# Fourteen Strassen blocks in place of eight plain ones in the first group of the second MLP

## Chip, cores and metric

The kernel runs on one core of a Trainium2 chip. The metric is the device time of one execution in microseconds; its median over three runs is shown, and one execution was profiled.

## The reference

A trunk of two layers works on 256 tokens of 2048 channels in float32. Layer 0 mixes by causal pooling, layer 1 by stick-breaking attention over shared keys and values; each ends in the same kind of MLP, with 8192 hidden channels, and the change concerns the MLP of layer 1.

```python
def rms_norm(x, g):
    xf = x.astype(jnp.float32)
    y = xf * lax.rsqrt(jnp.mean(xf * xf, axis=-1, keepdims=True) + EPS)
    return (y * g.astype(jnp.float32)).astype(x.dtype)

def squared_relu_mlp(x, w_up, w_down):
    h = jax.nn.relu(jnp.einsum('bsd,df->bsf', x, w_up))
    return jnp.einsum('bsf,fd->bsd', h * h, w_down)

def reference(...):
    for layer in range(DEPTH):
        if layer < N_A:
            x = x + multiscale_pool_mixer(rms_norm(x, pool_norm[layer]), pool_w[layer],
                                          pool_scale[layer])
        else:
            ...
            x = x + jnp.einsum('bsd,de->bse', o, w_o[j])
        x = x + squared_relu_mlp(rms_norm(x, mlp_norm[layer]), w_up[layer], w_down[layer])
    return rms_norm(x, final_norm)
```

## The kernel before

**Blocks and splits.** All weights pass through the core once, in blocks of 128 partitions x 4 x 512 (1 MB), listed in `order` beforehand. A product in float32 is made of three matmuls of a reduced type: activations and weights are each split into a high part and the rest (high x high, rest x high, high x rest). A block is therefore loaded (`load`), then split (`split`): ScalarE casts it into a tile `hi` (L194), VectorE subtracts that from the block into `lo` (L195). There are three buffers each for `hi` and `lo`, so a split may start when the block three places ahead of it has been multiplied. `next_block` keeps three blocks split and up to six loaded. Plain loads are issued by SyncE (L176) into three buffers `raw` or into one of four tiles `c0`, `c1`, `d0`, `d1`.

**Groups and Strassen's products.** The hidden channels of an MLP are worked in eight groups (`NG`) of 1024. Up-projections of groups 1 to 7 are made by seven products in Strassen's form (Winograd's variant): the 256 tokens and the group's two sets of 512 columns are halved, as are the 2048 input channels, and seven products on sums of quarters take the place of eight. Each product has two parts (input chunks 0 and 1, chunks 2 and 3), each with a block of its own: `P40` is product 4, part 0, and has 12 matmuls. The sums of weights are made while loading: product 4 loads a quarter into `c`; product 5 adds another quarter to it in the memory by an accumulating load, which POOL issues (L182), after product 4's block has been split; product 6 adds `d` to `c` on VectorE (L180); product 3 adds a third quarter by an accumulating load. Product 1 loads into `d`, and product 7 adds to that by an accumulating load. `c0` and `d0` serve part 0, `c1` and `d1` part 1. Product 2 loads a quarter of its own into `raw`. The table says so:

```python
CHAIN = {4: ("c", (1, 1)), 5: ("c", (1, 0)), 6: ("c", None), 3: ("c", (0, 1)),
         1: ("d", (0, 0)), 7: ("d", (1, 0)), 2: (None, (0, 1))}
```

**Group 0** of each MLP is made plainly (`whole`): eight blocks `U`, each with 24 matmuls (12 for each half of the tokens), into banks `x`, `y`, `z`, `turn`. It begins while the norm of input chunk 3 is still being made.

**A group's order** is written out in `stage_plan`. `T` are transposes of the activated hidden channels (four each, from tiles `c11` to `c22` into `ht0`, `ht1`), `D` are blocks of the down-projection of the group before (24 matmuls each). The first six groups of products begin as follows:

```python
        order = ("T0 T1 P40 T2 T3 P41" if g == 1 else "T2 P40 T3 P41 T0") + " P10 "
        order += ("" if g == 1 else "T1 ") + ("P11 D00 D01 P50 P51 D10 P60 P61 D11 D20 P70 P71 D21 "
                                              "P30 P31 D30 P20 P21 D31")
```

A planner places the instructions on each engine's queue at build time: by this order, but letting work that it takes to be ready go ahead of work that it takes to be waiting. On the chip every queue runs in the order so made.

**The norm.** Before the second MLP stands the output projection (16 blocks, `product_a`, L270 to L273). After each of its four chunks the norm's share of this chunk is made (`norm1.take`): squares (L316), transposes (L333), a scaling into a tile `f` (L414), casts and rests of quarters (L419, L420), sums of quarters (L425 to L431). The tiles `f` lie in `c0`, `c1`, `d0`, `c0`; a quarter that only the plain group 0 needs lies in `d1` (`other`). Chunk 3 is taken after the first block of group 0. The relu in the hidden channels scales by the token's factor (L492, L532).

Of the kernel before, what the change touches and what calls it, by code (L numbers as in the profile page):

```python
# [9 lines left out]
F32 = mybir.dt.float32  # L10
# [7 lines left out]
P = 128  # L18
# [3 lines left out]
NB = 512  # L22
NCH = D // NB
# [30 lines left out]
         1: ("d", (0, 0)), 7: ("d", (1, 0)), 2: (None, (0, 1))}  # L54


def stage_plan(g):


    if g == 0:  # L60
        order = "U000 U010 U001 U011 U100 U101 U110 U111"
    elif g < NG:
        order = ("T0 T1 P40 T2 T3 P41" if g == 1 else "T2 P40 T3 P41 T0") + " P10 "
        order += ("" if g == 1 else "T1 ") + ("P11 D00 D01 P50 P51 D10 P60 P61 D11 D20 P70 P71 D21 "
                                              "P30 P31 D30 P20 P21 D31")
        if g == NG - 1:
            order = order.replace("D11 D20 P70 P71 D21 P30 P31 D30 P20 P21 D31",
                                  "D11 P70 P71 D20 P30 P31 D21 P20 P21 D30")
    else:
        order = "T0 T1 E31 T2 T3 D00 D01 D10 D11 D20 D21 D30 D31"  # L70
    return [(s[0], *map(int, s[1:])) for s in order.split()]
# [3 lines left out]
def trunk_kernel(ctx: ExitStack, tc: tile.TileContext, xt_in, band, cols, pool_w, up_w, down_w,  # L75
# [60 lines left out]
    def mlp_blocks(layer):  # L136
        for g in range(NG + 1):
            last = {}
            for what, a, *b in stage_plan(g):
                if what in "DE":  # L140
                    block(down_w[layer, g - 1 - (what == "E"), a, b[0]])
                elif what == "U":
                    block(up_w[layer, g, a, b[0], b[1]])
                elif what == "P":
                    tag, at = CHAIN[a]
                    src = f"d{b[0]}" if at is None else up_w[layer, g, *at, b[0]]
                    last[a, b[0]] = block(src, tag=tag and f"{tag}{b[0]}", add=a in (5, 6, 3, 7),
                                          after=last[6, b[0]] if a == 7 else None)
# [58 lines left out]
    def next_block():  # L207
        while state["split"] < min(state["used"] + SPLITS, len(order)):
            split()
        while state["loaded"] < min(state["used"] + LOADS, len(order)):  # L210
            load()
        state["used"] += 1
        return ready.pop(0)
# [165 lines left out]
    class Fast(Norm):  # L379

        def __init__(self, gain, new_bank, homes):
            super().__init__()
            self.gain, self.new_bank, self.pools = gain, new_bank, []
            self.f, self.homes = [None] * NCH, homes

        def release(self):
            while self.pools:
# [5 lines left out]

        def quarters(self, n, src=None):

            if n == 0:
                self.other = wide("d1", F32R).rearrange("p n (l k s) -> p n l k s", l=2, k=2)
            pool = tc.alloc_tile_pool(name=f"fast{n}", bufs=1, side="right", reuse_waits="tile")  # L400
            self.pools.append(pool)
            hi = pool.tile([P, PARTS, 2, P], F32R, name="fh")
            lo = pool.tile([P, PARTS, 2, P], F32R, name="fl")
            self.parts[n] = (hi, lo)

            f = self.f[n] = wide(self.homes[n]).rearrange("p a (b k s) -> p (a b) k s", b=2, k=2)
            for half in range(2):
                if src is None:
                    bank = self.turned(n, half, (0, 1))
                for k in range(2):  # L410
                    c = 2 * half + k
                    x = bank[:, :, k, :] if src is None else src[:, c, :].rearrange(
                        "p (t s) -> p t s", t=NT)
                    nc.scalar.activation(out=f[:, 2 * half:2 * half + 2, k, :], in_=x, func=AF.Copy,  # L414
                                         scale=gt[:, self.gain, n * KT + c:n * KT + c + 1])
            for h, l, x in ((hi[:, 0], lo[:, 0], f[:, 0]),
                            (self.other[:, n, 0], self.other[:, n, 1], f[:, 1]),
                            (hi[:, 1:3], lo[:, 1:3], f[:, 2:4])):
                nc.scalar.copy(out=h, in_=x)  # L419
                nc.vector.tensor_tensor(out=l, in0=x, in1=h.bitcast(F32), op=ALU.subtract)  # L420

# [27 lines left out]
    def mlp(layer, norm, following, ps_s):  # L449

        with ExitStack() as later_pools:
# [8 lines left out]
            bank, u, h = {}, {}, {}  # L460
            r = None

            def product(i, part):

                name = {1: "x", 6: "x", 7: "x", 5: "y", 3: "y", 2: "z", 4: "z"}[i]
                begins = part == 0 and i in (1, 5, 2, 4)
                if begins:
                    bank[name] = ps_s.tile([P, NB], F32, name=name)
# [2 lines left out]
                for kg in range(2):  # L471
                    fh, fl = norm.parts[2 * part + kg]
                    for k in range(2):
                        ah, al = fh[:, SLOT[i], k, :], fl[:, SLOT[i], k, :]
                        wh, wl = hi[:, 2 * kg + k, :], lo[:, 2 * kg + k, :]
                        ends = part == 1 and kg == 1 and k == 1
                        nc.tensor.matmul(b, lhsT=ah, rhs=wh, start=begins and kg == 0 and k == 0,  # L477
                                         stop=False, skip_group_check=True)
                        nc.tensor.matmul(b, lhsT=al, rhs=wh, start=False, stop=False,  # L479
                                         skip_group_check=True)  # L480
                        nc.tensor.matmul(b, lhsT=ah, rhs=wl, start=False, stop=ends,  # L481
                                         skip_group_check=True)
                if part == 0:
                    return

# [80 lines left out]
            for g in range(NG + 1):  # L566
                follow = None
                if g == NG:
                    norm.release()
                    follow = following(new_bank)  # L570
                for what, *at in stage_plan(g):
                    if what == "P":
                        product(*at)
                    elif what == "T":
                        turn(*at, g == NG)
                    elif what == "U":
                        whole(*at)
                    elif what == "E":
                        down(*at)
                    else:  # L580
                        down(*at, follow)
# [3 lines left out]

    ps_s = four_banks(0)
    new_bank = bank_of(ps_s, ("z", "turn"))
    norm = Fast(G["mlp0"], new_bank, ("d0", "c0", "d0", "c1"))
    pools = [tc.alloc_tile_pool(name="xs23", bufs=1, reuse_waits="tile")]
    xs = [pools[0].tile([P, KT, S], F32, name=f"xs{n}") for n in range(2, NCH)]  # L590
    pp = tc.alloc_tile_pool(name="poolmix", bufs=2, reuse_waits="tile")
# [182 lines left out]
    for hg in range(NHG):  # L774
# [86 lines left out]
        product_w(kvq.parts, to_heads(qT, "q"))  # L861
        side.extend([[logs(0)], [logs(1)], [weights(0)], [weights(1)], [mix(0)], [mix(1)]])
        product_a(kvq.parts, to_values)
    norm1 = Fast(G["mlp1"], None, ("c0", "c1", "d0", "c0"))
    last_banks = []

    def end_of_attention():
        attention.close()
        ps_m[0].release()
        last_banks.append(four_banks(1))  # L870
        norm1.new_bank = bank_of(last_banks[0], ("z", "turn"))

    side.append([end_of_attention])
    for n in range(NCH):
# [4 lines left out]
        product_a(oT, added)  # L879
        if n < NCH - 1:  # L880
            norm1.take(n)
    op.release()
    side.append([lambda: norm1.take(NCH - 1)])


    class Last(Norm):
# [127 lines left out]
```

## Time and profile before

| what | us |
|---|---|
| median of three runs (1811.88 to 1813.05) | 1813.01 |
| the profiled execution | 1811.7 |
| its span, first to last instruction | 1810.0 |
| TensorE (PE) busy | 1797.5 |
| VectorE (DVE) busy | 1292.4 |
| ScalarE (ACT) busy | 1069.6 |
| GpSimd (POOL) busy | 92.5 |

Time lies mostly in the matmuls; a stage is read by cutting windows out of the span. The output projection ends at 1118.0 us of the span, group 0 of the second MLP runs to 1162.4, and each later group takes about 84 us.

### The profile page before, as it was taken

To read this page: it belongs to the slowest core of one execution; us is meant where nothing else is said; L and a number is where in the kernel's file an instruction comes from. 1 tells how busy PE (TensorE), PEld (TensorE's weight loads), DVE (VectorE), ACT (ScalarE), POOL (GpSimd) and SP (SyncE) were. 2 spreads that over 40 slices of the span, in tenths; PEclk is the share of its full clock that TensorE was granted. 3 is DMA by queue.
4 is the path that set the end of the run, shared out by engine and by line. 5 is a ranking of instruction groups with operands and counts; after the bars stand their busy time and mean duration, and the time that the engine had idled before them with its cause. 6 is when DMAs were issued, how large, how long until landed. Compare 5 with 4: busy or idle time off the path is not lost.

```text
span 1810.0 us, 20830 instructions
## 1 busy us (share of the span) xinstructions
PE 1797.5 (99%) x8348; PEld 1480.6 (82%) x8348; DVE 1292.4 (71%) x1098; ACT 1069.6 (59%) x1089; POOL 92.5 (5%) x125
## 2 busy tenths in 40 slices
PE   9999999999999999999999999999999999999998
PEld 4888888888888888888888888888888888888886
DVE  6577877877786876676766666577787868787863
ACT  5665665756565665565665555556565656566553
POOL 0000000000000100000000100000000101000000
PEclk9999999999999999999999999999999999999999
DMA  7678888897979874555445456797979798888851
GB/s 274 234 184 299 207 285 242 252 264 221 279 212 308 198 232 164 186 170 179 163 165 184 163 175 239 212 258 232 278 210 300 198 299 202 296 208 285 209 210 70
DMA packets 57553, 404.85 MB, mean 224 GB/s; under 512 B 6512, under 2 KB 6512, under 8 KB 9328
## 3 DMA queue, kind: packets, MB, share of 16 engines
q1 hardware_dynamic: 44784, 314.39, 47.7%
q0 software_dynamic: 12096, 88.09, 25.5%
q8 instruction: 65, 1.06, 0.2%
q10 hardware_dynamic: 576, 1.05, 0.2%
q14 instruction: 32, 0.26, 0.0%
HBM read 401.40 MB, written 2.10 MB: 223 GB/s over the span
## 4 chain that ended last, share of the span: by engine, by line
PE 98%; issue 1%; ACT 0%; DMA 0%; DVE 0%; SPq 0%; POOL 0%; ACTq 0%; POOLq 0%
PE bank L272 16%; PE bank L273 16%; PE bank L270 16%; PE bank L236 7%; PE x L477 4%; PE x L479 4%; PE x L481 4%; PE bank L241 3%; PE z L481 3%; PE z L477 3%; PE z L479 3%; PE y L481 3%; PE y L479 3%; PE y L477 3%; PE bank L683 2%; PE turn L545 1%
## 5 line engine op out<-in xcount | busy, mean ns | idle before, releaser
L195 DVE TENSOR_TENSOR lo<-raw,hi 128x2048 fp32r<-128x2048 f32 x188 | 430.6, 2290 | 247.4 <-ACT hi L194 246.9
L194 ACT CAST hi<-raw 128x2048 fp32r<-128x2048 f32 x188 | 359.6, 1913 | 305.8 <-PE bank L272 224.3
L272 PE MATMUL bank<-hi,ht 128*128 128x512 f32 x1024 | 399.9, 391 | 0.0
L273 PE MATMUL bank<-lo,ht 128*128 128x512 f32 x1024 | 399.3, 390 | 0.0
L270 PE MATMUL bank<-hi,ht 128*128 128x512 f32 x1024 | 399.3, 390 | 0.0
L195 DVE TENSOR_TENSOR lo<-c,hi 128x2048 fp32r<-128x2048 f32 x112 | 256.4, 2289 | 53.0 <-ACT hi L194 53.0
L194 ACT CAST hi<-c 128x2048 fp32r<-128x2048 f32 x112 | 214.6, 1916 | 126.4 <-PE bank L272 43.9
L272 PEld LDWEIGHTS bank<-hi,ht 128*128 128x128 f32 x1024 | 192.3, 188 | 44.0 <-DVE ht L550 4.6
L270 PEld LDWEIGHTS bank<-hi,ht 128*128 128x128 f32 x1024 | 192.3, 188 | 39.6
L273 PEld LDWEIGHTS bank<-lo,ht 128*128 128x128 f32 x1024 | 192.2, 188 | 39.4
L201 DVE SCALAR_TENSOR_TENSOR lo<-raw,gt,hi 128x512 fp32r<-128x512 f32 x192 | 135.4, 752 | 79.4 <-ACT hi L200 78.9
L200 ACT ACTIVATE hi<-raw,gt 128x512 fp32r<-128x512 f32 x192 | 126.0, 714 | 95.6 <-PE bank L236 48.5
L194 ACT CAST hi<-d 128x2048 fp32r<-128x2048 f32 x56 | 107.2, 1914 | 87.9 <-PE bank L272 67.2
L195 DVE TENSOR_TENSOR lo<-d,hi 128x2048 fp32r<-128x2048 f32 x56 | 128.3, 2292 | 42.7 <-ACT hi L194 42.7
L477 PE MATMUL x<-hi,fh 128*128 128x512 f32 x336 | 132.0, 393 | 0.0
L479 PE MATMUL x<-hi,fl 128*128 128x512 f32 x336 | 131.9, 393 | 0.0
L481 PE MATMUL x<-lo,fh 128*128 128x512 f32 x336 | 131.2, 390 | 0.0
L559 DVE TENSOR_TENSOR xr<-bank,xr 128x512 f32<-128x512 f32 x128 | 87.8, 686 | 39.8 <-PE bank L273 39.2
L182 POOL DMA_DIRECT2D c<-in_up_w x56 | 48.5, 866 | 875.8 <-DVE lo L195 829.8
L236 PE MATMUL bank<-d,hi 128*128 128x512 f32 x256 | 90.6, 398 | 0.0
L477 PE MATMUL z<-hi,fh 128*128 128x512 f32 x224 | 89.5, 400 | 0.0
L236 PE MATMUL bank<-c,hi 128*128 128x512 f32 x256 | 88.9, 395 | 0.0
(282 smaller groups left out, 2794.9 us busy)
## 6 DMA issues: line engine op xcount, KB each, us to landing
raw<-in_down_w SPq DMA_DIRECT2D x128, 1024.0 KB, 4.9
c<-in_up_w POOLq DMA_DIRECT2D x56, 1024.0 KB, 10.7
raw<-in_up_w SPq DMA_DIRECT2D x44, 1024.0 KB, 5.3
c<-in_up_w SPq DMA_DIRECT2D x28, 1024.0 KB, 5.1
d<-in_up_w SPq DMA_DIRECT2D x28, 1024.0 KB, 8.2
d<-in_up_w POOLq DMA_DIRECT2D x28, 1024.0 KB, 8.8
raw<-in_k_w SPq DMA_DIRECT2D x16, 1024.0 KB, 4.8
raw<-in_q_w SPq DMA_DIRECT2D x16, 1024.0 KB, 4.9
```

The source lines that it names most:

```text
L194: nc.scalar.copy(out=hi, in_=raw)
L195: nc.vector.tensor_tensor(out=lo, in0=raw, in1=hi.bitcast(F32), op=ALU.subtract)
L200: nc.scalar.activation(out=hi[:, k, :], in_=raw[:, k, :], func=AF.Copy, scale=gs)
L201: nc.vector.scalar_tensor_tensor(out=lo[:, k, :], in0=raw[:, k, :], scalar=gs, in1=hi[:, k, :].bitcast(F32), op0=ALU.mult, op1=ALU.subtract)
L236: nc.tensor.matmul(banks[j], lhsT=hi[:, k, cols], rhs=a, start=first, stop=last)
L270: nc.tensor.matmul(banks[t], lhsT=a_hi, rhs=hi[:, k, :], start=first and k == 0, stop=False)
L272: nc.tensor.matmul(banks[t], lhsT=a_lo, rhs=hi[:, k, :], start=False, stop=False)
L273: nc.tensor.matmul(banks[t], lhsT=a_hi, rhs=lo[:, k, :], start=False, stop=last and k == KT - 1)
L477: nc.tensor.matmul(b, lhsT=ah, rhs=wh, start=begins and kg == 0 and k == 0, stop=False, skip_group_check=True)
L479: nc.tensor.matmul(b, lhsT=al, rhs=wh, start=False, stop=False, skip_group_check=True)
L481: nc.tensor.matmul(b, lhsT=ah, rhs=wl, start=False, stop=ends, skip_group_check=True)
L559: nc.vector.tensor_tensor(out=chunk(t, n), in0=bank["d"][t], in1=chunk(t, n), op=ALU.add)
```

## The change

`stage_plan` gets the layer, and group 0 of the second MLP becomes fourteen Strassen blocks, part 0 of products 4, 1, 2 and 5 first. Product 2 takes bank `turn` in group 0, since `z` is still in use by product 4. `product` pops a side task behind each block, as `whole` does, so chunk 3's norm is taken behind `P40`. `next_block` stops loading where an accumulating load would have to wait for a split that isn't listed yet. The norm of the second MLP gets tiles of its own for `f` (`home`, in memory that attention has left, and `home1`, in memory of the attention's output), and doesn't make `other`; chunk 3's transposes go to banks of `ps_w`. The first MLP is as before.

```diff
-def stage_plan(g):
-    if g == 0:
+def stage_plan(layer, g):
+    if g == 0 and layer == 0:
         order = "U000 U010 U001 U011 U100 U101 U110 U111"
+    elif g == 0:
+        order = "P40 P10 P20 P50 P11 P41 P21 P51 P60 P61 P70 P71 P30 P31"
     elif g < NG:
...
         while state["loaded"] < min(state["used"] + LOADS, len(order)):
+            after = order[state["loaded"]][-1]
+            if after is not None and after >= state["split"]:
+                break
             load()
...
-        def __init__(self, gain, new_bank, homes):
+        def __init__(self, gain, new_bank, new_home, whole):
...
-            if n == 0:
+            if n == 0 and self.whole:
                 self.other = wide("d1", F32R).rearrange("p n (l k s) -> p n l k s", l=2, k=2)
...
-            f = self.f[n] = wide(self.homes[n]).rearrange("p a (b k s) -> p (a b) k s", b=2, k=2)
+            f = self.f[n] = self.new_home(n).rearrange("p a (b k s) -> p (a b) k s", b=2, k=2)
...
-            for h, l, x in ((hi[:, 0], lo[:, 0], f[:, 0]),
-                            (self.other[:, n, 0], self.other[:, n, 1], f[:, 1]),
-                            (hi[:, 1:3], lo[:, 1:3], f[:, 2:4])):
+            pieces = [(hi[:, 0], lo[:, 0], f[:, 0]), (hi[:, 1:3], lo[:, 1:3], f[:, 2:4])]
+            if self.whole:
+                pieces.insert(1, (self.other[:, n, 0], self.other[:, n, 1], f[:, 1]))
+            for h, l, x in pieces:
...
-            def product(i, part):
-                name = {1: "x", 6: "x", 7: "x", 5: "y", 3: "y", 2: "z", 4: "z"}[i]
+            def product(i, part, g):
+                name = {1: "x", 6: "x", 7: "x", 5: "y", 3: "y", 2: "z" if g else "turn", 4: "z"}[i]
...
+                after_block()
                 if part == 0:
                     return
...
-    norm1 = Fast(G["mlp1"], None, ("c0", "c1", "d0", "c0"))
-    last_banks = []
+    homes, last_banks = [], []
+    norm1 = Fast(G["mlp1"], None, lambda n: homes[-1].tile([P, KT, NB], F32, name="home"), False)
     def end_of_attention():
...
+        homes.append(tc.alloc_tile_pool(name="home", bufs=1, reuse_waits="tile"))
...
+    homes.pop().release()
     op.release()
-    side.append([lambda: norm1.take(NCH - 1)])
+    def last_taken():
+        later = tc.alloc_tile_pool(name="beside", bufs=1, reuse_waits="tile")
+        later.tile([P, KT, NB], F32, name="beside")
+        homes.append(tc.alloc_tile_pool(name="home1", bufs=1, reuse_waits="tile"))
+        norm1.new_bank = lambda: ps_w.tile([P, NB], F32, name="bank")
+        norm1.take(NCH - 1)
+        homes.pop().release()
+        later.release()
+    side.append([last_taken])
```

## Rows read from the trace of the kernel before

**Rows 1.** The page: busy time of each engine, share of the span, instructions.

```profile
PE 1797.5 (99%) x8348; PEld 1480.6 (82%) x8348; DVE 1292.4 (71%) x1098; ACT 1069.6 (59%) x1089; POOL 92.5 (5%) x125
```

**Rows 2.** Windows: stretch, length, busy us (instructions) by engine, clock, DMA share, GB/s.

```profile
1074.00:1118.00 44.00, 44.00 (x200) 36.22 (x199) 27.90 (x27) 23.19 (x32) 0.00 (x0) 1.00 0.64 230
...
1118.00:1162.40 44.40, 44.40 (x201) 36.87 (x200) 23.59 (x22) 21.92 (x25) 1.75 (x2) 1.00 0.70 231
```

**Rows 3.** Timeline of PE: start, us, engine, line, operation, out<-in, count.

```profile
1118.00 0.39 PE L525 MATMUL x<-hi,fh 128*128 128x512 f32 x1
...
1120.72 0.39 PE L525 MATMUL y<-hi,d 128*128 128x512 f32 x1
...
1123.44 0.60 PE L333 MATMUL z<-ident,xr 128*128 128x128 f32 x4
...
1162.44 0.39 PE L477 MATMUL z<-hi,fh 128*128 128x512 f32 x1
...
1164.96 0.66 PE L545 MATMUL turn<-ident,c 128*128 128x128 f32 x4
...
1168.58 0.48 PE L481 MATMUL z<-lo,fh 128*128 128x512 f32 x1
```

**Rows 4.** Groups of instructions by line and form, whole span.

```profile
L195 DVE TENSOR_TENSOR lo<-c,hi 128x2048 fp32r<-128x2048 f32 x112 | 256.4, 2289 | 53.0 <-ACT hi L194 53.0
...
L194 ACT CAST hi<-c 128x2048 fp32r<-128x2048 f32 x112 | 214.6, 1916 | 126.4 <-PE bank L272 43.9 <-PE x L479 26.3 <-PE y L479 22.3
...
L180 DVE TENSOR_TENSOR c<-c,d 128x2048 f32<-128x2048 f32 x28 | 64.0, 2286 | 0.4
...
L498 DVE TENSOR_TENSOR c<-y,c 128x512 f32<-128x512 f32 x14 | 9.6, 683 | 0.0
```

**Rows 5.** Timelines of DVE and POOL where group 1 begins.

```profile
1153.48 2.29 DVE L195 TENSOR_TENSOR lo<-c,hi 128x2048 fp32r<-128x2048 f32 x1 [3.15 <-ACT hi L194]
...
1156.07 0.89 POOL L182 DMA_DIRECT2D c<-in_up_w  x1 [126.34 <-DVE lo L195]
```

**Rows 6.** The page's loads: issuing queue, count, KB each, median us to landing.

```profile
c<-in_up_w POOLq DMA_DIRECT2D x56, 1024.0 KB, 10.7
...
c<-in_up_w SPq DMA_DIRECT2D x28, 1024.0 KB, 5.1
```

**Rows 7.** Landing of L182's loads: all, then those issued at 1156.07, 1245.27, 1196.23.

```profile
DMA to landing us min/median/max: 7.9/9.8/18.7
...
DMA to landing us min/median/max: 8.2/8.2/8.2
...
DMA to landing us min/median/max: 10.3/10.3/10.3
...
DMA to landing us min/median/max: 15.0/15.0/15.0
```

**Rows 8.** Timelines of ACT and DVE around the start of group 0.

```profile
1107.09 1.91 ACT L194 CAST hi<-raw 128x2048 fp32r<-128x2048 f32 x1 [2.58 <-PE bank L272]
...
1122.35 0.30 ACT L289 ACTIVATE rows<-total,eps 128x2 f32<-128x2 f32 x1 [1.81 <-DVE total L339]
...
1123.41 1.90 ACT L194 CAST hi<-raw 128x2048 fp32r<-128x2048 f32 x1 [0.52 <-PE y L527]
...
1109.03 2.29 DVE L195 TENSOR_TENSOR lo<-raw,hi 128x2048 fp32r<-128x2048 f32 x1 [2.01 <-ACT hi L194]
...
1119.95 2.29 DVE L195 TENSOR_TENSOR lo<-raw,hi 128x2048 fp32r<-128x2048 f32 x1 [1.07 <-ACT hi L194]
...
1127.89 0.42 DVE L420 TENSOR_TENSOR d<-c,d 128x256 fp32r<-128x256 f32 x1
```

**Rows 9.** Window of chunk 3's norm, VectorE alone: length, busy us (instructions), clock, DMA.

```profile
1122.20:1135.20 13.00, 9.19 (x16) 1.00 0.51 166
```

**Rows 10.** Windows at the end of the span, columns as in rows 2.

```profile
1797.00:1799.50 2.50, 0.00 (x0) 0.00 (x0) 1.12 (x7) 1.22 (x4) 0.00 (x0) 1.00 0.00 0
1799.50:1803.00 3.50, 3.14 (x15) 3.17 (x16) 1.91 (x5) 0.57 (x2) 0.00 (x0) 0.53 0.00 0
```

More of the change, by code (lines that the diff above doesn't have):

```diff
@@ L138, in mlp_blocks @@
             last = {}
-            for what, a, *b in stage_plan(g):
+            for what, a, *b in stage_plan(layer, g):
                 if what in "DE":
@@ L379, in trunk_kernel @@
     class Fast(Norm):
-        def __init__(self, gain, new_bank, homes):
+        def __init__(self, gain, new_bank, new_home, whole):
             super().__init__()
-            self.gain, self.new_bank, self.pools = gain, new_bank, []
-            self.f, self.homes = [None] * NCH, homes
+            self.gain, self.new_bank, self.pools, self.whole = gain, new_bank, [], whole
+            self.f, self.new_home = [None] * NCH, new_home
         def release(self):
@@ L570, in mlp @@
                     follow = following(new_bank)
-                for what, *at in stage_plan(g):
+                for what, *at in stage_plan(layer, g):
                     if what == "P":
-                        product(*at)
+                        product(*at, g)
                     elif what == "T":
@@ L587, in trunk_kernel @@
     new_bank = bank_of(ps_s, ("z", "turn"))
-    norm = Fast(G["mlp0"], new_bank, ("d0", "c0", "d0", "c1"))
+    norm = Fast(G["mlp0"], new_bank, lambda n: wide(("d0", "c0", "d0", "c1")[n]), True)
     pools = [tc.alloc_tile_pool(name="xs23", bufs=1, reuse_waits="tile")]
```

## The prediction

> **What bounds the kernel now.** I read the page first. TensorE is busy for 1797.5 of the 1810.0 us [rows 1], so on the whole only fewer matmuls, or a new wait of TensorE, can move the time. This busy share is a mean, though, and the change touches one stage: group 0 of the second MLP. So I cut the windows there next [rows 2]: TensorE has no gap, VectorE works 23.59 of 44.40 us, ScalarE 21.92. The timeline of TensorE then gives the scale [rows 3]. I call 1118.00 t = 0, the first matmul of the group. The twelve matmuls of one token half take 2.72 us (1118.00 to 1120.72), or 0.227 us each. The eight transposes of chunk 3's norm take 0.8 us. Group 1's first product begins at t = 44.4 (1162.44), and its second ends, four transposes of T0 and of T1 included, at about t = 50.9 (just behind 1168.58). The reader should see that one Strassen block (12 matmuls) occupies TensorE for 2.72 us and one plain block (24) for 5.44.
>
> **The gain.** Eight plain blocks are 192 matmuls, fourteen Strassen blocks 168. The 24 that go are worth 24 x 0.227 = 5.4 us. TensorE alone would end the group at 168 x 0.227 + 0.8 = t = 38.9.
>
> **What is added to the other engines.** Six more blocks have to be split: a cast of 1.92 us on ScalarE, then a subtraction of 2.29 on VectorE [rows 4]. P60 and P61 each add d to c on VectorE, 2.29 us each. Evacuations of the products add four VectorE operations of 0.68, and the dropped quarter saves 0.4. VectorE's work in the stage becomes 23.6 + 6 x 2.29 + 2 x 2.29 + 2.7 - 0.4 = 44.2 us, against 38.9 of TensorE. So VectorE by itself takes back the gain, unless work slides past the group's end. ScalarE comes to 21.9 + 6 x 1.92 = 33.4 us and a few copies, and bounds nothing.
>
> **The waits, which decide.** Six of the new loads are not plain: P50, P51, P70, P71, P30 and P31 add to a tile that an earlier block has just been split from. They can start only when that split has read the tile, and their own split only when they have landed. In group 1 this looks as follows [rows 5]: the subtraction of P40 starts at 1153.48 and ends at 1155.77, and POOL issues the accumulating load of P50 at 1156.07, 0.30 later. Its median time to landing is 10.7 us, while a plain load into c takes 5.1 [rows 6]. Alone it took 8.2, second of a close pair 10.3, third in a row with others beside it 15.0 [rows 7]. From the start of a cast to the end of its subtraction are 4.2 us (1107.09 to 1111.32) [rows 8]. Group 1 and the later groups put some 19 us of other blocks (two products, two down blocks, another product) between P41 and P51. The new list puts P21 alone between them, 2.72 us.
>
> So I follow tile c1 through the group: P41, P51, P61, P31, and then P41 of group 1. A block's third matmul needs the subtraction; ten matmuls, 2.27 us, follow it.
> - P41's split needs the buffers that P20 leaves: t = 3 x 2.72 + 0.8 = 9.0 at the earliest, so the subtraction ends at 13.2 at the earliest. But VectorE has chunk 3's norm ahead of it. In the stretch that holds this norm VectorE is busy 9.19 us, two subtractions (4.6) among them [rows 9]: 4.6 for the norm, 4.2 without the 0.42 of the dropped quarter [rows 8]. The subtraction of P20 ends at t = 4.2 (1119.95 + 2.29). In list order, P50's, P11's and P41's follow with the norm between: 4.2 + 4.2 + 3 x 2.29 = 15.3 without a gap. ScalarE has norm and casts to run in turn [rows 8], which makes some gaps. I take 16.0, between 13.2 and 17.2.
> - P51: 0.3 + 9.3 to landing (between alone and second of a pair, since P70's load and a plain one run beside it) + 4.2: t = 29.8. TensorE would want it at 20.3 (7 x 2.72 + 0.8 + 0.45).
> - P61: add 2.3, then 4.2: t = 36.3.
> - P31: third of three accumulating loads (P71, P30, P31, issued within some 5 us) with plain loads beside them. From 10.3 and 15.0 I take 12.6: 0.3 + 12.6 + 4.2 gives 53.4. The group ends at 55.7 instead of 44.4.
> - P41 of group 1 is a plain load into c1, once P31's split has read it: 0.3 + 5.1 + 4.2 gives 63.0, and the product ends at 65.3. Before it ended at 50.9. That is 14.4 us late. From there group 1 goes on as it does now, bound by TensorE, and nothing gives the time back.
>
> These waits cover others. P50 comes some 2 us late behind chunk 3's norm; P70 waits 1 us for the copy out of bank x; the transposes of T0 wait about 2 us for c12, now the last tile made (an addition of 0.68, a scaling, hand-overs). TensorE waits longer for c1 in each case. Without that cover they would cost up to 5 us, about what was gained.
>
> **Edits that I cost at nothing.** The quarters left out in chunks 0 to 2 save 0.4 us on each of VectorE and ScalarE in a stretch where TensorE has no gap [rows 2]. The homes lie where attention's tiles were, and chunk 3's in a dead part of oT; chunk 3's transposes take banks that the output projection had left. Without this cover a wait would show at the transposes, inside the 0.8 us. On SP's queue six plain loads replace eight, and c0, d0, d1 and c1 can be filled during the output projection. On POOL's queue P70's load stands behind P51's, which waits for P41's subtraction; but P70 is not due before P61. The break in the loading loop acts only where a base is one or two blocks back, so only in this group.
>
> **A rule against these rows.** An accumulating load of 1 MB took at least 7.9 us, over all of them [rows 7]. The Trainium skill (DMA: Bandwidth & Descriptors, Anatomy of one DMA) puts a load issued by GpSimd at about 2.0 us plus its bytes at 436 GB/s, an estimate of 4.4 us for 1 MB. By that P51 and P31 would come some 13 us earlier in all, and the sum would be within 2 us of before. The trace does not agree: 8.2 us, with nothing beside it.
>
> **The clock.** After 2.5 us without a matmul at the end, TensorE ran at a granted 0.53, nearly all at the lower level of 1.2 GHz, for 3.5 us [rows 10]. At P51 it waits 7 us or more. Each fall costs at most 3.5 us x half = 1.8, and only where TensorE sets the pace. In the likeliest case I add nothing, in the worst 2.
>
> **Rivals and chances.**
> - The likeliest, 0.47: the walk above, plus 9 to plus 19 us (1822 to 1832).
> - The same walk with little contention, 0.20: P41's subtraction at 13.2, loads at 8.2. P51 25.9, P61 32.4, P31 45.2, P41 of group 1 54.8, ended 57.1: plus 6.2, so 1819. For it: four of the loads begin on quiet queues. Against: the norm of chunk 3.
> - Worse, 0.13: 17.2, 10.3 and 15.0 together give 32.0, 38.5, 58.1, 67.7, ended 70.0: plus 19.1, with a fall of the clock plus 21, so 1834.
> - Faster or even, 0.12: the planner takes P41's split out of list order. It does move ready work ahead of waiting work: T0's transposes stand first in group 1's list and came behind eleven matmuls of P40 (1164.96) [rows 3]. If P41's subtraction ended by t = 6.9, 6.3 earlier than the floor of the second case, the chain would no longer cost anything. VectorE's 44.2 us then make it even (1813), or the whole 5.4 comes through, 1807.6, if its work slides into the down blocks behind. Against: the two buffers of a split come free one block at a time, and P50 and P11 are ready for them too. Faster 0.07, same 0.05.
> - Even, 0.08: the accumulating load lands nearly like a plain one, at 5.1. From 13.2 the walk gives 22.8, 29.3, 39.0, 48.6, ended 50.9, plus 0; from 16.0 plus 2.8 (1816). The rows speak against it [rows 7]. Same 0.06, faster 0.02. It is the case to which the rule of the Trainium skill above (DMA: Bandwidth & Descriptors, Anatomy of one DMA) points.
>
> **The numbers.** The profiled execution took 1811.7 us by its own clock, 1.7 beyond its span and 1.3 below the median of 1813.0. 1811.7 + 14.4 is 1826.1; by the median 1827.4, which I round to 1827. About 0.2%, 3.6 us, is what a measurement of this kernel can tell from no change. Slower by more: 0.47 + 0.20 + 0.13 = 0.80; within: 0.11; faster: 0.09. The range reaches from 1812, inside the even cases, to 1834, the worst: some 0.1 is left out on either side.
>
> **What the profile after would show.** Right: a wait of 6 to 10 us of TensorE at the third matmul of P51, ended by a subtraction on VectorE, which waits for a cast, which waits for an accumulating load into c; waits of a few us at P31 and at P41 of group 1; 24 matmuls fewer; groups 2 to 7 as long as before. Wrong: P51's load issued before t = 10, or landing in 5 us, or P41's split ahead of P50's. Then the group ends near t = 39 to 44, and the forecast fails at the walk of c1. If the group takes about 44 us with VectorE full, VectorE's work bounds it instead of the loads.

## The result and the profile after

The changed kernel takes 1833.64 us (median of four runs, 1832.99 to 1834.03), the kernel before 1812.45 on the same chip. The ratio is 1.0118, with a 95% interval of 1.0106 to 1.0130: 21.2 us slower. The profiled execution took 1833.58 us by its own clock, with a span of 1831.9.

The page of the changed kernel, answering to [rows 1], shows 24 matmuls fewer:

```profile
PE 1802.4 (98%) x8324; PEld 1479.8 (81%) x8324; DVE 1310.7 (72%) x1106; ACT 1081.0 (59%) x1095; POOL 97.7 (5%) x131
```

Windows of the changed kernel, columns as in [rows 2]: three of 25 us from the start of the stage, and one over a whole later group.

```profile
1118.00:1143.00 25.00, 21.02 (x94) 16.46 (x93) 18.64 (x20) 15.05 (x20) 1.73 (x2) 1.00 0.63 140
1143.00:1168.00 25.00, 12.75 (x38) 8.94 (x39) 12.17 (x6) 11.42 (x9) 2.59 (x3) 0.72 0.70 164
1168.00:1193.00 25.00, 23.09 (x96) 17.50 (x96) 18.10 (x13) 17.05 (x16) 1.73 (x2) 0.94 0.81 232
...
1266.90:1350.70 83.80, 83.80 (x378) 68.97 (x377) 64.42 (x41) 50.64 (x39) 5.20 (x6) 1.00 0.86 249
```

In the middle window TensorE works half of the time, and so do VectorE and ScalarE: no engine is the bound there. Over the three, TensorE is idle for 75 - 56.85 = 18.15 us; before it had no gap in the same stretch. The later group is without a gap, as before.

The first matmul of group 1's first down block (D00) marks the end of what changed. Timelines of TensorE, first the kernel before, then the changed one:

```profile
1175.32 0.39 PE L270 MATMUL bank<-hi,ht 128*128 128x512 f32 x1
```

```profile
1195.94 0.39 PE L275 MATMUL bank<-hi,ht 128*128 128x512 f32 x1
```

The stage's first matmul starts at 1118.00 before [rows 3] and at 1118.28 now. So D00 comes 77.7 us into the stage instead of 57.3: 20.3 us of the 21.9 between the two profiled executions. Times t below count from 1118.28.

What TensorE waits for between 1118 and 1195 (releaser, us in total, times, longest):

```profile
PE y L483 <- ACT hi L196: 6.9, 1, 6.9
PE x L483 <- ACT c L503: 5.8, 1, 5.8
PE x L487 <- DVE lo L197: 2.6, 2, 1.6
PE z L487 <- DVE lo L197: 1.2, 2, 0.9
PE x L483 <- ACT hi L196: 0.8, 2, 0.6
PE turn L552 <- ACT c L499: 0.5, 1, 0.5
PE z L483 <- ACT hi L196: 0.3, 1, 0.3
```

That is 18.1 us. TensorE's timeline puts the two long ones at P51 and at P70; the third line is the first matmul of group 1:

```profile
1147.23 0.79 PE L483 MATMUL y<-hi,fh 128*128 128x512 f32 x1 [6.88 <-ACT hi L196]
...
1167.53 0.79 PE L483 MATMUL x<-hi,fh 128*128 128x512 f32 x1 [5.79 <-ACT c L503]
...
1180.60 0.50 PE L483 MATMUL z<-hi,fh 128*128 128x512 f32 x1 [0.27 <-ACT hi L196]
```

**The wait at P51** is followed back through three queues: POOL (the adding loads of P51, P71, P31), ScalarE, VectorE.

```profile
1135.97 0.86 POOL L184 DMA_DIRECT2D c<-in_up_w  x1 [5.00 <-DVE lo L197]
...
1154.44 0.86 POOL L184 DMA_DIRECT2D d<-in_up_w  x1 [1.57 <-PE y L487]
1159.39 0.86 POOL L184 DMA_DIRECT2D c<-in_up_w  x1 [4.09 <-DVE lo L197]
```

```profile
1145.28 3.70 ACT L196 CAST hi<-c 128x2048 fp32r<-128x2048 f32 x2 [6.59 <-DMA c<-in_up_w]
...
1154.39 0.59 ACT L503 COPY c<-y 128x512 f32<-128x512 f32 x1 [4.78 <-PE y L487]
1154.87 1.91 ACT L196 CAST hi<-c 128x2048 fp32r<-128x2048 f32 x1
...
1165.09 1.90 ACT L196 CAST hi<-d 128x2048 fp32r<-128x2048 f32 x1 [6.52 <-DMA d<-in_up_w]
1166.90 0.58 ACT L503 COPY c<-x 128x512 f32<-128x512 f32 x1
```

```profile
1127.28 2.29 DVE L182 TENSOR_TENSOR c<-c,d 128x2048 f32<-128x2048 f32 x1
...
1133.16 2.29 DVE L197 TENSOR_TENSOR lo<-c,hi 128x2048 fp32r<-128x2048 f32 x1
...
1147.21 4.49 DVE L197 TENSOR_TENSOR lo<-c,hi 128x2048 fp32r<-128x2048 f32 x2 [6.05 <-ACT hi L196]
1151.62 2.28 DVE L182 TENSOR_TENSOR c<-c,d 128x2048 f32<-128x2048 f32 x1
1156.81 2.29 DVE L197 TENSOR_TENSOR lo<-c,hi 128x2048 fp32r<-128x2048 f32 x1 [2.90 <-ACT hi L196]
...
1174.48 2.29 DVE L197 TENSOR_TENSOR lo<-c,hi 128x2048 fp32r<-128x2048 f32 x1 [2.89 <-ACT hi L196]
...
1184.88 2.29 DVE L197 TENSOR_TENSOR lo<-c,hi 128x2048 fp32r<-128x2048 f32 x1 [1.62 <-ACT hi L196]
```

Read it as one chain: VectorE finishes P41's split (1133.16 + 2.29), POOL issues P51's load at 1135.97, ScalarE waits 6.59 us for it and casts from 1145.28, and TensorE starts P51 when the first of the two casts is done. VectorE meanwhile waits 6.05 us for ScalarE. No engine is busy; all wait for one transfer.

**The wait at P70** has its cause in the order of ScalarE's queue: the copy that empties bank `x` (1166.90) stands behind the cast of P71's block (1165.09), which waits 6.52 us for its load. TensorE needs the copy, not yet the cast. P71's load in turn went out at 1154.44, 0.54 us behind the end of P61's addition (1151.62 + 2.28), and that addition had waited for P51's split: this wait hangs on `c1` too.

How long the three adding loads issued at 1135.97, 1154.44 and 1159.39 took to land:

```profile
DMA to landing us min/median/max: 9.2/9.2/9.2
...
DMA to landing us min/median/max: 10.6/10.6/10.6
...
DMA to landing us min/median/max: 13.0/13.0/13.0
```

**The clock.** Windows behind the two long waits:

```profile
1147.20:1153.90 6.70, 6.08 (x14) 4.30 (x15) 6.69 (x3) 2.41 (x2) 0.86 (x1) 0.50 0.21 18
1167.50:1171.20 3.70, 3.67 (x9) 2.91 (x10) 3.70 (x2) 1.77 (x1) 0.00 (x0) 0.52 1.02 281
```

The granted clock is 0.50 and 0.52 there, the lower level of 1.2 GHz. Matmuls stand 0.43 us apart instead of 0.227, and the first one behind a wait 0.60: that makes 3.2 us over the first stretch and 1.7 over the second, 4.9 in all.

The balance up to D00: -5.4 (matmuls) + 18.1 (waits) + 4.9 (clock) = 17.6 of 20.3 us. The rest is in TensorE's timeline too. The step into a wait and the step behind it take some 0.1 to 0.2 us more than the wait itself and 0.227 us (P51's first matmul comes 7.26 us behind P21's last, 6.88 of them waiting): 2.3 us more than before, added up. The transposes, in more pieces, take 0.5 us more.

### The profile page after: what moved, and what is told of

Its sections match the earlier page's. It is cut to its first block, busy times and chain, and to the rows that moved or that the text cites. A ratio compares the mean times of both kernels' runs of the same rounds, so it can differ in the third digit from the quotient of the medians.

```text
span 1831.9 us, 20815 instructions
## 1 busy us (share of the span) xinstructions
PE 1802.4 (98%) x8324; PEld 1479.8 (81%) x8324; DVE 1310.7 (72%) x1106; ACT 1081.0 (59%) x1095; POOL 97.7 (5%) x131
## 4 chain that ended last, share of the span: by engine, by line
PE 96%; DMA 1%; issue 1%; ACT 1%; DVE 1%; SPq 0%; POOL 0%; ACTq 0%; POOLq 0%
PE bank L277 16%; PE bank L275 16%; PE bank L278 16%; PE bank L241 7%; PE x L483 4%; PE x L485 4%; PE x L487 4%; PE bank L246 3%; PE y L487 3%; PE y L485 3%; PE y L483 3%; PE z L487 3%; PE z L483 3%; PE z L485 3%; PE bank L690 2%; PE turn L552 1%
## 5 line engine op out<-in xcount | busy, mean ns | idle before, releaser
L197 DVE TENSOR_TENSOR lo<-raw,hi 128x2048 fp32r<-128x2048 f32 x182 | 416.8, 2290 | 231.0 <-ACT hi L196 230.5
L196 ACT CAST hi<-raw 128x2048 fp32r<-128x2048 f32 x182 | 348.2, 1913 | 291.3 <-PE bank L277 216.7
L197 DVE TENSOR_TENSOR lo<-c,hi 128x2048 fp32r<-128x2048 f32 x120 | 274.7, 2290 | 61.2 <-ACT hi L196 61.1
L196 ACT CAST hi<-c 128x2048 fp32r<-128x2048 f32 x120 | 229.7, 1915 | 131.6 <-PE bank L277 46.4
L483 PE MATMUL x<-hi,fh 128*128 128x512 f32 x360 | 143.0, 397 | 6.6 <-ACT c L503 5.8
L487 PE MATMUL x<-lo,fh 128*128 128x512 f32 x360 | 141.3, 392 | 2.6 <-DVE lo L197 2.6
L485 PE MATMUL x<-hi,fl 128*128 128x512 f32 x360 | 142.2, 395 | 0.0
L483 PE MATMUL y<-hi,fh 128*128 128x512 f32 x240 | 94.5, 394 | 6.9 <-ACT hi L196 6.9
L485 PE MATMUL y<-hi,fl 128*128 128x512 f32 x240 | 94.3, 393 | 0.0
L487 PE MATMUL y<-lo,fh 128*128 128x512 f32 x240 | 94.1, 392 | 0.0
```

Of the source, the lines that this page charges most:

```text
L196: nc.scalar.copy(out=hi, in_=raw)
L197: nc.vector.tensor_tensor(out=lo, in0=raw, in1=hi.bitcast(F32), op=ALU.subtract)
```

## Experiments

The theory: six loads that add to a tile just split, and land late, set the pace. Rivals: VectorE's work; the order on ScalarE's queue alone; the low clock; the edits beside. Each kernel is compared with the kernel before on its own chip (1812.0 to 1812.8 us). "D00" is the time from the stage's first matmul to D00's in the profiled execution, read as above.

| kernel | median us | ratio, 95% | D00 at us |
|---|---|---|---|
| before | 1812.45 | | 57.3 |
| after | 1833.64 | 1.0118 (1.0106 to 1.0130) | 77.7 |
| 1 group 0 plain again | 1811.98 | 1.0001 (0.9992 to 1.0010) | 57.3 |
| 2 plain loads into raw | 1809.52 | 0.9986 (0.9977 to 0.9995) | 54.5 |
| 3 the same without the two sums | 1809.16 | 0.9985 (0.9976 to 0.9994) | 54.0 |
| 4 copies on VectorE | 1832.50 | 1.0114 (1.0100 to 1.0128) | 79.1 |
| 5 P51's load plain | 1824.81 | 1.0069 (1.0054 to 1.0084) | 69.7 |
| 6 P71's load plain | 1828.96 | 1.0092 (1.0075 to 1.0109) | 73.8 |
| 7 P41 earlier | 1825.68 | 1.0072 (1.0057 to 1.0087) | 71.1 |
| 8 filler matmuls | 1835.68 | 1.0129 (1.0113 to 1.0145) | 78.1 |
| 9 products 5 and 7 unchained | 1827.15 | 1.0084 (1.0069 to 1.0099) | 70.6 |
| 10 is 7 and 4 | 1824.58 | 1.0064 (1.0047 to 1.0080) | 69.7 |
| 11 plain loads in place | 1824.90 | 1.0069 (1.0052 to 1.0086) | 69.8 |
| 12 product 5 alone unchained | 1820.66 | 1.0046 (1.0031 to 1.0061) | 64.4 |

The time of the profiled execution less its D00 lies between 1754.4 and 1755.9 us in all fourteen kernels, so what these edits do to the time happens before D00.

**1. Group 0 plain again, everything else as changed.**

```diff
-    if g == 0 and layer == 0:
+    if g == 0:
...
-    norm1 = Fast(G["mlp1"], None, lambda n: homes[-1].tile([P, KT, NB], F32, name="home"), False)
+    norm1 = Fast(G["mlp1"], None, lambda n: homes[-1].tile([P, KT, NB], F32, name="home"), True)
```

> The new tiles for f, and chunk 3's banks, with group 0 in its eight plain blocks again (and the quarter that they need made again). If these edits cost nothing, as the prediction had it: the time of before within 0.1%, 1811 to 1814 us. If one of them carries part of the 21 us, such as a wait of chunk 3's tile for the output projection: 1815 us or more, with a gap of TensorE at the transposes of chunk 3.

Measured: 1811.98 us, no wait of TensorE in the stage. The tiles and banks cost nothing; the loss comes with the fourteen blocks. The loading rule isn't tested here: with group 0 plain no adding load stands that close to the block it adds to, and no run sets the rule apart. In the changed kernel no cast of the stage waits for a plain load into `raw`, so no delay by it is seen.

**2. The six adding loads made plain**, from SyncE into `raw`.

```diff
+                    if layer == 1 and g == 0 and (a, b[0]) in ((5, 0), (5, 1), (3, 0), (3, 1), (7, 0), (7, 1)):
+                        last[a, b[0]] = block(src)
+                        continue
                     last[a, b[0]] = block(src, tag=tag and f"{tag}{b[0]}", add=a in (5, 6, 3, 7),
```

> In group 0 of the second MLP, P50, P51, P70, P71, P30 and P31 load their quarter plainly into the buffers of raw instead of adding it to a tile just split; so the sums of weights of products 5, 6, 7 and 3 lack terms. Number of splits, additions on VectorE and matmuls stay. If the accumulating loads make the waits: the group ends near t = 44 (VectorE's 44.2 us of work), P41 of group 1 some 6 us later, and the time is 1809 to 1816 us. If VectorE's and ScalarE's added work makes them, whatever the loads: little changes, 1828 us or more.

TensorE's waits in the stage, and two windows:

```profile
PE y L486 <- ACT hi L199: 1.8, 1, 1.8
PE y L490 <- DVE lo L200: 0.6, 1, 0.6
```

```profile
1118.00:1143.00 25.00, 24.40 (x111) 19.92 (x111) 23.52 (x23) 21.29 (x24) 0.00 (x0) 1.00 0.60 227
1143.00:1168.00 25.00, 23.25 (x103) 18.51 (x103) 21.64 (x13) 19.89 (x16) 1.76 (x2) 1.00 0.96 320
```

The waits fall from 18.1 to 2.4 us and the granted clock is 1.00 in both windows. The adding loads, with their place behind the splits, carry 24 us (1833.6 - 1809.5). D00 comes 2.8 us sooner than before, with 2.4 of waits: 5.2, so the gain of 5.4 is there. VectorE is busy 23.52 of 25 us and still delays TensorE hardly at all.

**3. Experiment 2, and P60 and P61 split `d` as it is, without the sum of `c` and `d`.**

```diff
+                    if layer == 1 and g == 0 and (a, b[0]) in (..., (6, 0), (6, 1)):
...
+        if base is None and isinstance(src, str):
+            raw = raws[src]
```

> As the run with plain loads, and P60 and P61 split the tile d as it stands, without the addition of c on VectorE: 4.6 us of VectorE's work less, so 39.6 against 38.9 of TensorE. If VectorE's 44.2 us bound the run with plain loads: 3 to 5 us faster than that run, 1806 to 1810. If something else bounds it (latency of single splits): within 1 us of that run.

4.6 us less on VectorE bring 0.4 us (1809.16 against 1809.52), inside the measurement. VectorE doesn't bound this stage even when the loads are out of the way.

**4. The four copies out of the banks on VectorE instead of ScalarE.**

```diff
-                    nc.scalar.copy(out=new({4: "21", 1: "11", 5: "22", 6: "12"}[i]), in_=b)
+                    dst = new({4: "21", 1: "11", 5: "22", 6: "12"}[i])
+                    if layer == 1 and g == 0:
+                        nc.vector.tensor_copy(dst, b)
+                    else:
+                        nc.scalar.copy(out=dst, in_=b)
```

> The four copies out of the banks in group 0 go to VectorE instead of ScalarE, so that the copy out of bank x after P61 no longer stands behind the cast of P71, which waits for an accumulating load. If this queue order makes the second wait: the wait of 5.8 us before P70 goes, but P71's and P31's loads land no earlier, so TensorE waits for them instead, and the time falls by 1 to 4 us, to 1829 to 1833. If the queue order were the whole second loss (5.8 us and the lower clock behind it): 7 us or more, 1827 or less.

```profile
PE y L483 <- ACT hi L196: 6.8, 1, 6.8
PE x L483 <- ACT hi L196: 3.9, 2, 3.4
PE x L487 <- DVE lo L197: 3.6, 3, 1.5
```

The wait for the copy is gone (5.8 to 0.9), the time isn't: TensorE waits for the casts instead. P71's and P31's loads come as late as before. 1832.50 us is 1.1 less than the changed kernel, inside the first expectation but within what two measurements may differ by.

**5 and 6. One adding load alone made plain**, P51's and then P71's, by the edit of experiment 2 with the list ((5, 1),) and ((7, 1),).

> Of the six accumulating loads P51's alone becomes a plain load into raw (its sum of weights lacks a term; P61 then adds d1 to what P41 loaded). If the chain P41, P51, P61 through tile c1 sets the pace, everything behind P51 comes earlier: the wait of 6.9 us and the lower clock behind it go, P61's addition and P71's and P31's loads begin some 10 us sooner: 8 to 14 us less, 1820 to 1826. If the waits behind P51 stand on their own (P71's load, queue order), they grow by what the first wait gave: 4 us less at most, 1829 or more.

> P71's load alone becomes plain, into raw. If the second wait (5.8 us before P70, because the copy out of bank x stands behind P71's cast on ScalarE, which waits for this load) is a cause of its own: 6 to 8 us less, 1826 to 1828. If c1 is the pace and P31's accumulating load, whose subtraction ends at t = 58.5, is next in line: TensorE waits there instead, 1 to 3 us less, 1831 to 1833.

P51 plain: 8.8 us less than the changed kernel. The wait at P51 shrinks to 0.8 and a longer one stands at P30, whose load is one of three that POOL now issues between 1140.57 and 1147.54:

```profile
1159.66 0.79 PE L486 MATMUL y<-hi,fh 128*128 128x512 f32 x1 [9.68 <-ACT hi L199]
```

P71 plain: 4.7 us less, between the two expectations. The wait at P70 is gone, the one at P51 is as it was, and 1.75 us stand at P30:

```profile
1147.36 0.79 PE L486 MATMUL y<-hi,fh 128*128 128x512 f32 x1 [6.98 <-ACT hi L199]
...
1163.80 0.49 PE L486 MATMUL y<-hi,fh 128*128 128x512 f32 x1 [1.75 <-ACT hi L199]
```

The waits aren't independent: with one load made plain, the next one in line (P30's, into `c0`) sets the pace, so neither edit gives its whole wait back.

**7. P41 and P60 further forward.**

```diff
-        order = "P40 P10 P20 P50 P11 P41 P21 P51 P60 P61 P70 P71 P30 P31"
+        order = "P40 P10 P20 P11 P41 P50 P21 P60 P51 P61 P70 P71 P30 P31"
```

> Another order of the same fourteen blocks: P40 P10 P20 P11 P41 P50 P21 P60 P51 P61 P70 P71 P30 P31, with three blocks between P41 and P51 in place of one. If the accumulating loads' latency over the few blocks between is the cause: P41's subtraction ends at t = 14 instead of 17, three blocks cover most of P51's load, and the group ends 6 to 12 us sooner, 1821 to 1828. If the number of accumulating loads on the DMA engines or VectorE's work bounds the group, the order doesn't matter: within 3 us of 1833.

8.0 us less, as expected. TensorE no longer waits at P51; the wait at P70 stays, 7.4 us sooner than the changed kernel's (1167.53):

```profile
1160.08 0.79 PE L483 MATMUL x<-hi,fh 128*128 128x512 f32 x1 [5.99 <-ACT c L503]
```

**8. Filler matmuls into an unused bank, 30 ahead of P51 and 24 ahead of P70**, to keep TensorE at work where it waits.

```diff
+                for _ in range({(5, 1): 30, (7, 0): 24}.get((i, part), 0) if layer == 1 and g == 0 else 0):
...
+                    nc.tensor.matmul(bank["idle"], lhsT=onesr, rhs=norm.parts[0][0][:, 0:2], start=True,
+                                     stop=True)
```

> The changed kernel with matmuls into an unused bank ahead of P51 (30) and of P70 (24), so that TensorE has work in the two long waits. The result is the same. If the lower clock behind the waits costs on the path: 14 and 8 matmuls come back to 0.227 us from 0.43, 2 to 4 us less, 1829.5 to 1831.5. If the loads alone set the pace, the faster matmuls only wait longer further on: within 1 us of 1833.6. If the matmuls come late they delay P51: slower.

1835.68 us, not faster than the changed kernel. The fillers went out in pieces, only partly in the gaps, and the clock fell all the same behind the first gap, to a mean of 0.71 (first line). Behind the second it stayed at full (second line), and TensorE waits 1.23 us for the subtraction at P31's third matmul in its place (last line), where the changed kernel has no wait:

```profile
1150.00:1160.00 10.00, 9.97 (x32) 7.96 (x33) 7.25 (x4) 4.27 (x4) 2.02 (x3) 0.71 0.62 116
1160.00:1170.00 10.00, 8.39 (x37) 6.51 (x36) 4.17 (x3) 4.19 (x3) 0.58 (x1) 1.00 1.01 239
```

```profile
1178.09 0.50 PE L492 MATMUL y<-lo,fh 128*128 128x512 f32 x1 [1.23 <-DVE lo L197]
```

So the second fall, taken away, brought nothing here; what the first one costs stays open.

**9. Products 5 and 7 unchained**: each sum in a buffer of its own, by a plain load and an adding load right behind it; product 4 into `raw`.

```diff
+                    if layer == 1 and g < 2 and a in ((4, 5, 7) if g == 0 else (4, 5)):
+                        two = {4: up[1, 1, b[0]], 5: (up[1, 1, b[0]], up[1, 0, b[0]]),
+                               7: (up[0, 0, b[0]], up[1, 0, b[0]])}[a]
+                        last[a, b[0]] = block(two, tag=f"c{b[0]}" if a == 5 else None)
+                        continue
...
-            nc.sync.dma_start(raw, src)
+            nc.sync.dma_start(raw, src[0] if isinstance(src, tuple) else src)
+            if isinstance(src, tuple):
+                nc.gpsimd.dma_start(raw, src[1], accum_op=ALU.add)
...
-        order = "P40 P10 P20 P50 P11 P41 P21 P51 P60 P61 P70 P71 P30 P31"
+        order = "P40 P10 P20 P50 P11 P21 P51 P60 P61 P41 P70 P71 P30 P31"
```

> The same fourteen products with the same sums, but P50, P51, P70 and P71 make their sum in a buffer of its own: a plain load, then an accumulating one behind it, so neither waits for a split (P40 and P41 load plainly into raw; so in group 1). The order is P40 P10 P20 P50 P11 P21 P51 P60 P61 P41 P70 P71 P30 P31, with four blocks between P6 and P3 of a tile. Six accumulating loads stay, and four plain loads are added. If the waits come from loads that start only behind a split: they go, and the time is near that of the run with plain loads, 1808.5 to 1813. If the six accumulating loads themselves, by what they take of the DMA engines, hold the group up: 1820 or more.

1827.15: the time of the second theory (1820 or more), not of the first. The wait at P51 is gone, but P70 waits 6.0 us, again for a copy behind P71's cast, and that cast waits for the adding load, issued at 1143.47 and landed 13.5 us later:

```profile
1157.12 1.90 ACT L204 CAST hi<-raw 128x2048 fp32r<-128x2048 f32 x1 [8.64 <-DMA raw<-in_up_w]
```

```profile
1143.00:1168.00 25.00, 16.63 (x55) 12.41 (x54) 12.88 (x6) 12.77 (x10) 1.73 (x2) 0.80 1.01 297
```

The DMA engines are full (share 1.01) over these 25 us. That alone doesn't make the wait: in experiment 2 they were busy for 0.96 of the same stretch. A sum without a chain costs a load more, and product 7's holds one of three `raw` buffers through both transfers; which of these makes the load late isn't shown.

**10. Experiments 7 and 4 together.**

> The order of the run with P41 earlier (1825.7), and the four copies of group 0 on VectorE. There TensorE's longest wait, 6.0 us, is for the copy out of bank x behind a cast that waits for P71's load. If that wait is now a cause of its own: 4 us less or more, 1821.5 or below. If P71's load, behind P61's addition, is the pace whichever engine copies: within 2 us of 1825.7.

1824.58, 1.1 us from experiment 7 alone, as the second expectation had it: with the order changed too, it doesn't matter which engine copies.

**11. The chains kept, the adding taken out**: the six loads overwrite the tile, from POOL, behind the same split.

```diff
+    first = len(order) + 12 * NCH + 4 * NCH
...
+                if first <= i < first + 14:
+                    nc.gpsimd.dma_start(raw, src)
+                else:
+                    nc.gpsimd.dma_start(raw, src, accum_op=ALU.add)
```

> All blocks, waits, buffers and queues as in the changed kernel, but the six loads of group 0 that add to a tile (P50, P51, P70, P71, P30, P31) overwrite it, from the same queue and still behind the split that reads the tile; the sums of weights of products 5, 6, 7 and 3 of this group lack terms. Plain loads from SyncE took 5.1 us by the median, the adding ones 8.0 to 13.0. Theory 1, the slow landing is nearly all of it: P51's split comes 3.5 to 4 us sooner, P71's some 5 and P31's some 7, the waits of 6.9 and 5.8 us before P51 and P70 shrink to under 3 and 1, and the time is 1812 to 1817. Theory 2, it is the waiting behind a split that costs, however fast the load then lands: the wait before P51 stays above 4 us, and the time is 1820 to 1828.

The landing of P51's load, TensorE's longest waits, and where the longest stands:

```profile
DMA to landing us min/median/max: 5.1/5.1/5.1
```

```profile
PE z L487 <- ACT hi L200: 2.8, 1, 2.8
PE y L487 <- ACT hi L200: 2.7, 1, 2.7
PE x L491 <- DVE lo L201: 2.6, 2, 1.6
```

```profile
1172.33 0.50 PE L487 MATMUL z<-hi,fh 128*128 128x512 f32 x1 [2.83 <-ACT hi L200]
```

All six loads land in 5.0 to 5.3 us. The waits at P51 and P70 shrink to 2.7 and 0.7, as theory 1 said, but the time is 1824.9, which theory 2 said. So each has a part: of the 24 us that experiment 2 takes away, taken in this order, the slow landing of an adding load is 8.7 (1833.6 - 1824.9), and its place behind the split, in one tile, 15.4 (1824.9 - 1809.5). The second share holds whatever else experiment 2 changes: the issuing queue, the buffer, and the loading rule that no longer acts. TensorE still waits 11.4 us, in smaller pieces, at P51, at product 6 and at the first product of group 1 among others; the load of that product into c0 can't start before P30's split has read the tile.

**12. Product 5 alone unchained**, by the edit of experiment 9 with `a in (4, 5)`; product 7 adds to `d` as before.

> Products 4 and 5 of groups 0 and 1 get loads that wait for no split: product 4 loads into raw, product 5 loads plainly into c and adds its second quarter there at once; product 7 still adds to d behind the split of product 1, so raw isn't held for long. Order P40 P10 P20 P50 P11 P21 P51 P60 P61 P41 P70 P71 P30 P31. Theory 1, the chain behind splits is the cause, and the full unchaining failed only for the raw buffers that it held: the waits before P51 (6.9) and P70 (5.8) are both under 2 us, and the time is 1813 to 1819. Theory 2, adding loads are too slow whatever they wait for, since they crowd the transfers: a wait of 4 us or more stands at some other block, and the time is 1823 to 1830.

1820.66, the best of the versions that leave nothing out, and still slower than before. No wait is left at P51, as theory 1 said, and 2.8 us at P70, between its 2 and theory 2's 4; the time, too, lies between both, nearer to theory 1's. One of the adding loads of group 1, issued at 1170.68, took this long to land, and the DMA engines are full:

```profile
DMA to landing us min/median/max: 17.9/17.9/17.9
```

```profile
1143.00:1168.00 25.00, 19.88 (x72) 15.48 (x73) 16.72 (x9) 16.05 (x12) 1.16 (x2) 0.86 1.02 302
```

Product 5 unchained, with the new order, takes 13 us of the loss away. Experiment 7 took 8 by an order alone, so the share of the chain by itself isn't shown. That transfers are the next limit is argued, not shown: P71's load still waits for P61's addition, and experiment 2 had the engines busy for 0.96 of this stretch with hardly a wait.

## Why the prediction was right, and where its size was off

The direction and the place were right: TensorE waits at P51 (6.9 us; 6 to 10 forecast) for a cast that waits for an adding load, VectorE idle, and groups 2 to 7 as before. The wait stands at P51's first matmul, for the cast, not at the third for the subtraction, as I had it. The waits that I forecast at P31 and at P41 of group 1 are not in the list; the second long wait was at P70, where I had put 1 us. The size was 14.4 us forecast, 21.2 measured. 1833.6 lies outside the likeliest case and at the upper end of the range, in the time of the rival "worse". Of that rival's conditions, P41 at 17.2 and the fall of the clock came, the long landings didn't, so that the time still lies inside the range is in part luck. The walk of c1, in t:

| step | forecast | measured | lag added |
|---|---|---|---|
| P41's subtraction ends | 16.0 | 17.2 (1133.16 + 2.29) | 1.2 |
| P51's ends | 29.8 | 31.2 (half of the two from 1147.21) | 0.2 |
| P61's ends | 36.3 | 40.8 (1156.81 + 2.29) | 3.1 |
| P31's ends | 53.4 | 58.5 (1174.48 + 2.29) | 0.6 |
| P41's of group 1 ends | 63.0 | 68.9 (1184.88 + 2.29) | 0.8 |
| P41 of group 1 multiplied | 65.3 | 71.5 | 0.3 |

The lags add up to 6.2 us: P41 of group 1 ends 20.6 us late instead of 14.4, and D00 comes 20.3 late.

- **The gain** of 5.4 us: held (experiment 2, 5.2).
- **"VectorE by itself takes back the gain unless work slides"**: failed. The added work is there (VectorE's busy time rises by 18.3 us over the whole execution), but with the loads plain D00 comes sooner than before, and 4.6 us less of it change nothing (experiment 3). The work does slide.
- **The landings**: held. 9.2 and 13.0 us measured, 9.3 and 12.6 assumed.
- **P61 = add 2.3, then 4.2**: this is the term that was mis-sized, 3.1 us. I let the add follow P51's subtraction at once. VectorE's queue had P60's subtraction in between (the x2 at 1147.21), some 2.1 us; and P61's cast stood on ScalarE behind the copy of bank `y`, some 1.0 us, since P51 ran at half clock and emptied late. At 0.227 us a matmul, an estimate from the third one at 1150.05, P51 would have ended at 1152.3, before the addition did (1153.90).
- **"P70 waits 1 us for the copy out of bank x"**: failed, 5.8. I counted the copy itself, not what stands ahead of it on ScalarE: a cast that waits for a load. Up to P31 the chain of c1 covers most of it, as I said of such waits: from P70's start at t = 49.3, 48 matmuls (10.9) and 1.7 of low clock give 61.9 for the end of P31, about 1 us later than c1's 58.5 + 2.27. That 1 us isn't in the table, since the load of group 1's P41 waits for P31's split, not for its matmuls.
- **The clock at nothing**: failed as a count of TensorE's time (4.9 us). By the rows the first fall reached the chain of c1 with the 1.0 us above; how much of the whole reached the end stays open (experiment 8).
- **Edits costed at nothing**: held for the tiles and banks (experiment 1); the loading rule has no run of its own.
- **The planner**: P41's split was not brought ahead of P50's; P60's add (1127.28) and subtraction were brought forward, ahead of P41's subtraction and of P61's add, and each made c1 later. P70's load went out at 1130.10, ahead of P51's and not behind it.

**The rule against these rows.** An adding load of 1 MB took 8.0 us here with nothing close to it (P50's, issued at 1111.91), the three shown above 9.2, 10.6 and 13.0; a plain one from the same queue took 5.0 to 5.3 (experiment 11). The 8.2 us that I had taken for a load alone were not quite that: the next adding load went out 5.4 us behind it, at 1161.51. The Trainium skill (DMA: Bandwidth & Descriptors, Anatomy of one DMA) gives 4.4 us as an estimate for 1 MB issued by GpSimd: the plain loads come near it, the adding ones don't. Even with 5 us the chains would have kept 12.7 us of loss (1824.9 - 1812.2), where the forecast's walk gave 0 to 2.8. With such loads the walk is short by more, then. From P41's 17.2 it gives 26.8, 33.3, 42.9 and, for group 1's P41, 52.5; the trace of experiment 11 has 27.0, 36.9, 47.3 and 60.1. P61's term fails there too, by 3.4 us, and P41 of group 1 adds 3.2; the plain loads into `c` ahead of group 1 took 7.3 and 7.9 us in that trace, not 5.1.

## What to carry to other kernels

A list that saves matmuls must also be read as chains through each buffer: split, load that adds, split again; the number of other blocks between two links decides, and here one block of 2.72 us stood where the later groups have some 19 us (experiment 7: 8.0 us for another order of the same blocks). On each engine's queue look for the instruction that TensorE needs and that stands behind one waiting for a transfer. And ask first what the change can bring at best: here, with the six loads made plain, 2.5 us, 0.14%.

## What the runs showed of the hardware

- Adding into the memory costs a 1 MB load about 3 us of latency when alone (8.0 against 5.0 to 5.3 from the same queue). Beside other loads it took up to 17.9 us (experiment 12); plain loads from SyncE, too, took up to 14.2 us in the trace before, against a median of 5.0, so no row shows that company costs an adding load more.
- After idle stretches of 6.9 and 5.8 us TensorE ran at 1.2 GHz for 6.7 and 3.7 us; in the first of them P51 ended late, and behind it the copy out of its bank and the next cast on ScalarE.
